# A router-and-experts stage: gathered rows that carry their weights, and a rarely taken block cut in two

## The chip, the cores and the metric

The kernel runs on one core of one Trainium2 chip. The metric is the device time of one execution in microseconds (us), taken as the median of several runs. Engine names are those of the profile: PE (matrix multiply, with PEld for its weight loads), DVE, ACT, POOL and SP; PEq, DVEq and so on are the engines' instruction sequencers.

## The reference

The program is a network over 256 tokens of width 1024: two layers of mixer and grouped mixture of experts, then two more blocks of attention, cross attention and feed-forward. The change touches the mixture of experts, which runs once in each of the first two layers:

```
def grouped_moe(h, router_w, router_b, w_gate, w_up, w_down):
    t = h.reshape(B_ * S, D)
    scores = jax.nn.sigmoid((t @ router_w).astype(jnp.float32))
    sel = scores + router_b.astype(jnp.float32)
    ...
    top_s = jnp.take_along_axis(scores, top_idx, axis=-1)
    top_w = top_s / jnp.sum(top_s, axis=-1, keepdims=True)
    combine = jnp.einsum('nk,nke->ne', top_w, jax.nn.one_hot(top_idx, N_EXPERTS, dtype=jnp.float32))
    y = jnp.zeros((t.shape[0], D), jnp.float32)
    for e in range(N_EXPERTS):
        he = jax.nn.silu(t @ w_gate[e]) * (t @ w_up[e])
        y = y + combine[:, e:e + 1] * (he @ w_down[e]).astype(jnp.float32)
```

The router picks one of four groups and two of the four experts in it. There are 16 experts with gate and up matrices of 1024 x 512 and a down matrix of 512 x 1024, all float32: 96 MB of weights in each layer.

## The kernel before

`moe(l)` (L1229) is one such stage. It normalises x into xn (two tiles of 128 tokens), splits xn into a high and a low part (xh on ACT, xl on POOL, L1274, in `parts`), computes the router's scores on PE and the choice on DVE (sel, pair, ec, gc, pick, L1291 to L1317), ranks each token within its expert (rk, L1327), and counts the tokens of each expert. The counts, as integers in the tile cnti (L1338), are read into registers, because the code branches on them. POOL also writes xn to a DRAM tile xd (L1289) from which rows are gathered later.

The experts are worked off in eight pairs p, each with room for 64 tokens of either expert. The tokens of the pairs 0 and 1 (`FIRST` is 2) are brought together by one-hot matmuls (`gather`, ph, L1374); from pair 2 on POOL gathers rows of xd by an index list (`rows`, L1419), and `columns` turns them on PE into hg. `tokens_of` (ohb, L1391) makes the one-hot masks from which `indices` computes the lists. Then `up(p)` multiplies with gate and up (pg, pu, L1474, 64 matmuls), adds the previous pair's result to x (scatter, py, L1510 and L1511), forms hd = silu(pg) * pu (L1484, L1485), transposes it, and builds the pair's placing matrix Sm and its combine weights ws in `places` (two transposes pS and four small products pw on PE, copies on ACT). `down(p)` multiplies with the down matrices (po, L1523).

A pair has twelve weight loads of 1 MB, issued by SP in program order (`fetch`, L222) into a rotation of 17 slots; each waits until its slot is free.

More than 64 tokens for an expert are handled by branches. In `more_up` and `more_down` (L1671, L1674) a pair gets a second pass for 32 further tokens of each expert; in the runs shown this happens once, in layer 0 for pair 3. Whatever still exceeds that is done by `rest` (L1609), a long block under `tc.If(left > 96)` that passes every token through every expert. It is never taken in these runs, so each engine named in it jumps over it once in each layer, in pair 5 between up and py:

```
                left = nc.values_load(cnti[0:1, 0:1], min_val=0, max_val=2 * S, engines=engines + (mybir.EngineType.SP,))
                with tc.If(left > 96):
```

PE, DVE, ACT and SP take part. Inside are both token tiles and 16 experts, 912 matmuls and transposes on PE in all, with weights fetched by SP into four slots of the rotation that are set aside for it (`self.spare`); the gate and up loads of pair 6 are issued ahead of it for that reason. What follows the block on an engine waits until the jump is over.

Of the kernel before, what the change touches and what calls it, by code (L numbers as in the profile page):

```python
# [11 lines left out]
F32 = mybir.dt.float32  # L12
# [9 lines left out]
P = 128  # L22
# [98 lines left out]
class Net:  # L121
# [99 lines left out]
    def fetch(self, raw, src, rows="(k p) n -> p k n"):  # L221
        self.nc.sync.dma_start(raw, src.rearrange(rows, p=P))  # L222
        return raw
# [1005 lines left out]
    def moe(self, l):  # L1229
# [4 lines left out]
        with self.phase(f"moe{l}", MOE_RING, True) as mp:  # L1234
# [14 lines left out]
            xh = mp.tile([P, 2, D], F32R, name="xh")  # L1249
            xl = mp.tile([P, 2, D], F32R, name="xl")  # L1250
# [28 lines left out]
            xd = self.dram.tile([S, D], F32, name="xd")  # L1279
# [9 lines left out]
            nc.gpsimd.dma_start(xd.rearrange("(t p) d -> p t d", p=P), xn)  # L1289
# [59 lines left out]
            self.split(cs, ch, cl)  # L1349
            def hot(ps, c0, n):  # L1350
# [3 lines left out]
                for t in range(2):  # L1354
                    if m == 4:
                        oh = kept[:, t, :].rearrange("p (e s) -> p e s", e=m)
                    else:
                        oh = mp.tile([P, m, n], F32R, tag=f"oh{m}{t}", name="oh")
# [5 lines left out]
            hg = []  # L1364
# [18 lines left out]
            ones_of, idx, got = [], mp.tile([P, 16], I32, name="idx"), []  # L1383
# [13 lines left out]
            def indices():  # L1397
                px = self.bank([P, 16], name="px")
                for p in range(2, 8):
                    h, q = (p - 2) // 3, (p - 2) % 3  # L1400
                    for c, n, col in ((0, 128, p), (128, 64, 8 + p)):
                        for t in range(2):
                            mm(px[0:n, col:col + 1], ones_of[2 * h + t][:, q, c:c + n], self.tok[:, t:t + 1],
                               start=t == 0, stop=t == 1)

                none = mp.tile([P, 16], F32, name="none")
                for n, c in ((P, 2), (64, 10)):
                    e = (slice(0, n), slice(c, c + 6))
                    V.tensor_scalar(none[e], px[e], 0.5, 2.0 * S, op0=ALU.is_lt, op1=ALU.mult)
                    V.scalar_tensor_tensor(idx[e], px[e], -1.0, none[e], op0=ALU.add, op1=ALU.add)  # L1410
                got.extend(mp.tile([P, 2, D], F32, tag=n, name=n) for n in ("xh", "xl"))
# [4 lines left out]
            def rows(i, p):  # L1416

                n = 64 if i else 128
                nc.gpsimd.indirect_dma_start(got[i][0:n, p % 2, :], None, xd[:, :],  # L1419
                                             bass.IndirectOffsetOnAxis(ap=idx[0:n, 8 * i + p:8 * i + p + 1], axis=0),  # L1420
                                             bounds_check=S - 1, oob_is_err=False)

            def columns(src, n, out):

                src = src.rearrange("r (b q k) -> r b k q", b=2, k=4)
                for b in range(2):
                    pt = self.bank([P, 4, n], name="hgT")
# [11 lines left out]
            def places(oh, p, r):  # L1439
# [7 lines left out]
                Sm = kept[:, 3 if r else 2, :]  # L1447
                if not r:
                    ws = mp.tile([P, 1], F32, tag="ws", name="ws", bufs=3)
                else:  # L1450
                    ws = mp.tile([P, 1], F32, tag="wsa", name="wsa")
                nc.scalar.copy(Sm, pS)  # L1452
                m = 32 if r else 64
                for i in range(P // m):
                    e = 2 * p + i % 2
                    nc.scalar.copy(ws[m * i:m * i + m, :], pw[m * i:m * i + m, e:e + 1])
                return Sm, ws

            def up(p, W, between=None):

                nonlocal oneh
                if p == 0:
                    oneh = hot((0, 1), 0, 64)
# [20 lines left out]
                nc.scalar.activation(hd, pg, AF.Silu)  # L1484
                V.tensor_tensor(hd, hd, pu, op=ALU.mult)  # L1485
# [4 lines left out]
                Sm, ws = places([oneh[t][:, q] for t in range(2)], p, 0)  # L1490
                if 1 <= p < 7:
                    columns(got[0][:, (p + 1) % 2, :], P, hg[0][:, (p + 1) % 2])
# [4 lines left out]
                if p in (1, 3, 5):  # L1497
                    oneh = hot((p + 1, p + 2), 0, 64)
                return hidT, Sm, ws

            def turn_hidden(hd, out):
                pt = self.bank([P, 4, P], name="hT")
# [47 lines left out]
            def more_up(p, W, hidT):  # L1550

                oh = hot((p,), 64, 32)
                hga = self.sp.tile([P, KD, 64], F32, tag="e1", name="hga")
                columns(got[1][0:64, p % 2, :], 64, hga)
# [6 lines left out]
                twice = self.sp.tile([P, 2, 2, 64], F32R, tag="gt", name="ohd")  # L1561
                for t in range(2):
                    V.tensor_copy(twice[:, t], oh[t].unsqueeze(1).to_broadcast([P, 2, 64]))
                Sm, ws = places([twice[:, t].rearrange("p c s -> p (c s)") for t in range(2)], p, 1)
# [32 lines left out]
            def weights(src, step, p, into=None):  # L1597
                w = I[src][l, 2 * p], I[src][l, 2 * p + 1]
                n = w[0].shape[1]
                into = [t.rearrange("p (k n) -> p k n", n=n) for t in into or [self.slot([P, 2048]) for i in range(4)]]  # L1600
# [8 lines left out]
            def rest():  # L1609


                W.extend(first_two(6))
                self.spare = [self.slot([P, 2048]) for i in range(4)]
                left = nc.values_load(cnti[0:1, 0:1], min_val=0, max_val=2 * S, engines=engines + (mybir.EngineType.SP,))
                with tc.If(left > 96):
                    n = 0
                    wv = mp.tile([P, 16], F32, name="wv")
                    ft = self.spare[0][:, 0:1024]
                    hc = self.spare[0][:, 1024:2048].rearrange("p (k n) -> p k n", n=P)
                    hid = self.spare[0][:, 0:512].rearrange("p (k n) -> p k n", n=P)  # L1620
                    for t in range(2):
                        V.tensor_scalar(wv[:, 0:2 * FIRST], rk[:, t, 0:2 * FIRST], 64.0, None, op0=ALU.is_gt)
                        V.tensor_scalar(wv[:, 2 * FIRST:], rk[:, t, 2 * FIRST:], 96.0, None, op0=ALU.is_gt)
                        V.tensor_tensor(wv, wv, cs[:, t, :], op=ALU.mult)
                        nc.sync.dma_start(ft, xd[128 * t:128 * t + 128, :])
                        columns(ft, P, hc)
                        for e in range(NE):
                            ps = []
                            for src in ("exp_w_gate", "exp_w_up"):
                                ps.append(self.bank([P, 512], name="pe"))  # L1630
                                for b in range(2):
                                    w = self.spare[1 + n % 3].rearrange("p (k n) -> p k n", n=512)
                                    n += 1
                                    self.fetch(w, I[src][l, e][512 * b:512 * b + 512, :], "(p k) n -> p k n")
                                    for k in range(4):
                                        mm(ps[-1], hc[:, 4 * b + k, :], w[:, k, :], start=b + k == 0, stop=b + k == 4)
                            hd = self.sp.tile([P, 512], F32, tag="gt", name="hde")
                            nc.scalar.activation(hd, ps[0], AF.Silu)
                            V.tensor_tensor(hd, hd, ps[1], op=ALU.mult)
                            turn_hidden(hd, hid)  # L1640
                            po = [self.bank([P, 512], name="poe") for c in range(2)]
                            for b in range(2):
                                w = self.spare[1 + n % 3].rearrange("p (k n) -> p k n", n=D)
                                n += 1
                                self.fetch(w, I["exp_w_down"][l, e][256 * b:256 * b + 256, :], "(p k) n -> p k n")
                                for k in range(2):
                                    for c in range(2):
                                        mm(po[c], hid[:, 2 * b + k, :], w[:, k, 512 * c:512 * c + 512], start=b + k == 0,
                                           stop=b + k == 2)
                            for c in range(2):  # L1650
# [815 lines left out]
```

## Time and profile before

| | |
|---|---|
| runs | 1595.86, 1598.49, 1601.05 us (median 1598.49) |
| profiled execution | 1595.95 us, span 1594.2 us |
| PE busy | 1497.0 us (94%) |
| DVE / ACT / POOL busy | 915.6 (57%) / 677.5 (42%) / 149.7 us (9%) |
| moved by DMA | 417.80 MB, mean 262 GB/s |
| expert stage of layer 0 / layer 1 | about 195 to 460 us / 600 to 850 us |

All times are us from the start of the span. In a row of the timeline, the brackets give the idle time of the engine just before, and what ended it. "PEclk" is the clock that PE was granted, as a share of full speed. A jump, a register read and a semaphore wait are no work: they show in the list of waits and under their line of the program, on the sequencers.

### The profile page before, as it was taken

The page shows a single profiled execution, that of the slowest core. Times are in us where ns is not written, and L with a number is a line of the kernel's source. Part 1 is how long each engine was busy: PE and PEld are TensorE (multiplying, and loading weights), DVE is VectorE, ACT ScalarE, POOL GpSimd, SP SyncE. Part 2 cuts the span into 40 slices and gives each one's busy share as a digit, 9 for nine tenths or more (in the row PEclk, how much of TensorE's full clock was granted, in tenths as well). Part 3 has the DMA queues.
Part 4 walks back from the last instruction along what each step waited for, and adds up shares of the span by engine and source line. Part 5 has one row for each costly group of instructions (what it writes and reads, how often), then busy time and mean ns, then how long its engine had stood idle before and what let it go on. Part 6 is the DMA issues. An engine that isn't in the chain of part 4 may idle for free.

```text
span 1594.2 us, 23071 instructions
## 1 busy us (share of the span) xinstructions
PE 1497.0 (94%) x8797; PEld 1065.8 (67%) x8797; DVE 915.6 (57%) x1773; ACT 677.5 (42%) x1417; POOL 149.7 (9%) x196
## 2 busy tenths in 40 slices
PE   6999979998989997999898999999999999999998
PEld 3666634434459974444345887788887997788886
DVE  4755533233358984223216786866667777766665
ACT  3434431111145643111115354765556666665554
POOL 0320011000000002100001100110000211110000
PEclk9999999999989998999999999999999999999999
DMA  9998989999958887999998532555644443545540
GB/s 356 349 312 297 361 334 408 420 405 385 401 185 264 292 335 296 412 419 420 416 370 270 179 108 92 171 186 172 220 163 162 160 144 95 182 162 196 200 158 27
DMA packets 171642, 417.80 MB, mean 262 GB/s; under 512 B 9588, under 2 KB 93196, under 8 KB 146928
## 3 DMA queue, kind: packets, MB, share of 16 engines
q1 hardware_dynamic: 165696, 403.46, 68.5%
q0 software_dynamic: 5536, 12.51, 2.3%
q8 instruction: 86, 1.41, 0.4%
q14 instruction: 52, 0.43, 0.1%
q10 hardware_dynamic: 272, 0.00, 0.0%
HBM read 418.79 MB, written 3.16 MB: 265 GB/s over the span
## 4 chain that ended last, share of the span: by engine, by line
PE 40%; DVE 4%; DMA 2%; ACT 2%; issue 1%; POOL 1%; DVEq 0%; POOLq 0%; SPq 0%; ACTq 0%
PE pgu L2341 9%; PE pgu L2342 5%; PE fy L383 2%; PE fy L382 2%; PE fy L381 2%; PE lin L381 2%; PE lin L382 2%; PE lin L383 2%; DMA w<-in_exp_w_up 1%; PE sc L911 1%; PE linc L381 1%; DVE hl L230 1%; PE op L383 1%; PE op L381 1%; PE linc L382 1%
## 5 line engine op out<-in xcount | busy, mean ns | idle before, releaser
L230 DVE TENSOR_TENSOR hl<-w,hl 128x1024 fp32r<-128x1024 f32 x280 | 336.1, 1233 | 51.5 <-ACT hl L229 51.3
L229 ACT CAST hl<-w 128x1024 fp32r<-128x1024 f32 x280 | 280.2, 1046 | 33.3 <-DMA w<-in_even_w_in 19.9
L2341 PE MATMUL pgu<-hT,hl 128*128 128x512 f32 x640 | 224.4, 393 | 0.0
L2342 PE MATMUL pgu<-hT,hl 128*128 128x256 f32 x640 | 178.3, 279 | 0.0
L381 PE MATMUL lin<-hl,hThi 128*128 128x256 f32 (+2 forms) x480 | 160.1, 336 | 2.4 <-ACT hl L229 1.8
L382 PE MATMUL lin<-hl,hThi 128*128 128x256 f32 (+2 forms) x480 | 154.8, 323 | 1.8 <-DVE hl L230 1.7
L383 PE MATMUL lin<-hl,hTlo 128*128 128x256 f32 (+2 forms) x480 | 153.6, 321 | 0.0
L2341 PEld LDWEIGHTS pgu<-hT,hl 128*128 128x128 f32 x640 | 120.0, 187 | 27.0
L1485 DVE TENSOR_TENSOR hd<-hd,pu 128x512 f32<-128x512 f32 x16 | 11.0, 688 | 214.2 <-PE pu L1474 214.2
L1474 PE MATMUL pg<-w,hg 128*64 128x512 f32 x512 | 117.7, 611 | 13.9 <-ACT hg L1378 10.1
L2342 PEld LDWEIGHTS pgu<-hT,hl 128*128 128x128 f32 x640 | 120.7, 189 | 2.0
L1523 PE MATMUL po<-w,hidT 128*64 128x512 f32 x512 | 116.6, 605 | 3.8 <-PEq L1674 1.8
L1474 PE MATMUL pu<-w,hg 128*64 128x512 f32 x512 | 114.3, 593 | 2.2 <-DMA w<-in_exp_w_up 2.2
L381 PEld LDWEIGHTS lin<-hl,hThi 128*128 128x128 f32 x480 | 93.4, 195 | 18.0 <-issue 7.9
L382 PEld LDWEIGHTS lin<-hl,hThi 128*128 128x128 f32 x480 | 93.6, 195 | 10.8 <-DVE hl L230 3.2
L1474 PEld LDWEIGHTS pg<-w,hg 128*64 128x64 f32 x512 | 42.4, 141 | 85.2 <-issue 58.1
L383 PEld LDWEIGHTS lin<-hl,hTlo 128*128 128x128 f32 x480 | 93.2, 194 | 7.2 <-DVE hl L230 0.8
L1474 PEld LDWEIGHTS pu<-w,hg 128*64 128x64 f32 x512 | 41.9, 137 | 71.4 <-issue 65.6
L1523 PEld LDWEIGHTS po<-w,hidT 128*64 128x64 f32 x512 | 42.9, 139 | 66.4 <-issue 61.2
L1452 ACT CAST kept<-pS 128x256 fp32r<-128x256 f32 x17 | 6.3, 373 | 170.0 <-PE pS L184 170.0
L1538 ACT CAST eo<-of 128x512 fp32r<-128x512 f32 x32 | 19.8, 617 | 115.5 <-DVE of L1535 115.2
L381 PE MATMUL linc<-hThi,hl 128*128 128x256 f32 x224 | 66.8, 298 | 0.0
(573 smaller groups left out, 2930.2 us busy)
## 6 DMA issues: line engine op xcount, KB each, us to landing
w<-in_exp_w_gate SPq DMA_DIRECT2D x64, 1024.0 KB, 15.1
w<-in_exp_w_down SPq DMA_DIRECT2D x64, 1024.0 KB, 14.5
w<-in_exp_w_up SPq DMA_DIRECT2D x64, 1024.0 KB, 15.7
w<-in_ada_w SPq DMA_DIRECT2D x48, 1024.0 KB, 7.8
w<-in_ffn_wg SPq DMA_DIRECT2D x22, 1024.0 KB, 5.5
w<-in_ffn_wu SPq DMA_DIRECT2D x22, 1024.0 KB, 7.4
w<-in_ffn_wd SPq DMA_DIRECT2D x22, 1024.0 KB, 8.7
w<-in_even_w_in SPq DMA_DIRECT2D x14, 1024.0 KB, 10.2
```

The source lines that it names most:

```text
L229: pin(self.nc.scalar.copy(w[:, 0], src))
L230: pin(self.nc.vector.tensor_tensor(w[:, 1], src, w[:, 0].bitcast(F32), op=ALU.subtract))
L381: pin(mm(out, lh, rh, start=start, stop=False))
L382: pin(mm(out, lh, rl, start=False, stop=False))
L383: pin(mm(out, ll, rh, start=False, stop=stop))
L911: pin(self.nc.tensor.matmul(p[:, os], q[:, qs], k[:, ks], start=os.start > 0, stop=False))
L1474: pin(mm(pp[64 * j:64 * j + 64, :], hg[0][:, p % 2, k, 64 * j:64 * j + 64], w[j][k // 4][:, k % 4, :], start=k == 0, stop=k == KD - 1, til ...
L1485: V.tensor_tensor(hd, hd, pu, op=ALU.mult)
L1523: pin(mm(po[c][64 * j:64 * j + 64, :], hidT[:, k, 64 * j:64 * j + 64], W[2][j][k // 2][:, k % 2, 512 * c:512 * c + 512], start=k == 0, sto ...
L1538: nc.scalar.copy(eh[c], of)
L2341: mm(pp[i], wh[:, k, :], both[:, :, k, :], start=k == 0, stop=False)
L2342: mm(pp[i][:, 0, :], wl[:, k, :], hi[:, k, :], start=False, stop=k == KD - 1)
```

## The change

1. xd is written earlier. Each token tile of xn goes to DRAM right behind its normalisation, as a DMA of its own on POOL's queue, pinned in program order, ahead of `parts`. Rows of xd have 16 further columns, into which the combine weights cs are written by a third DMA; the gathered rows bring their weights along. Gathers are 128 rows wide also for the second pass.
2. From pair 2 on `places` is replaced by `known`: Sm is one comparison on DVE of the slot numbers with the token number of each row, and ws is copied by ACT out of the gathered row. The one-hot tiles of the later pairs go.
3. `tokens_of` does three comparisons for each mask instead of two.
4. `rest` becomes two blocks, for one token tile each, in pairs 5 and 6. Their weights would be fetched by POOL into the gather tiles, so SP and the rotation have no part in them, and the loads of pair 6 are issued like all others. PE, DVE, ACT and POOL take part.
5. Silu and the product hd are pinned in program order.

```
 def fetch(self, raw, src, rows="(k p) n -> p k n", by=None):
-        self.nc.sync.dma_start(raw, src.rearrange(rows, p=P))
+        (by or self.nc.sync).dma_start(raw, src.rearrange(rows, p=P))
...
+            xd = self.dram.tile([S, D + NE], F32, name="xd")
             for t in range(2):
                 for k0 in (0, 4):
                     self.norm_cols(self.norm_turn(self.x, t, k0), hT, t, k0)
                 rs[t] = self.norm_rows(self.x, t, xn, t)
-            xd = self.dram.tile([S, D], F32, name="xd")
+                pin(nc.gpsimd.dma_start(xd[128 * t:128 * t + 128, 0:D], xn[:, t, :]))
             parts(0)
...
             parts(1)
-            nc.gpsimd.dma_start(xd.rearrange("(t p) d -> p t d", p=P), xn)
...
             self.split(cs, ch, cl)
+            nc.gpsimd.dma_start(xd[:, D:].rearrange("(t p) e -> p t e", p=P), cs)
...
-                        o = self.sp.tile([P, 3, 192], BF16, tag=("e2", "gt")[h], name="ohb")
+                        o = self.sp.tile([P, 3, 256], BF16, tag=("e2", "gt")[h], name="ohb")
...
-                        for c, n, s0 in ((0, 64, 0), (128, 32, 64)):
+                        for c, n, s0 in ((0, 64, 0), (128, 32, 64), (192, 32, 64)):
...
+            def known(p, i, Sm):
+                V.tensor_scalar(Sm, slots, number[:, 6 * i + p:6 * i + p + 1], None, op0=ALU.is_equal)
+                ws = mp.tile([P, 1], F32, tag=("ws", "wsa")[i], name="ws", bufs=(3, 1)[i])
+                m = 32 if i else 64
+                for g in range(P // m):
+                    h, e = slice(m * g, m * g + m), D + 2 * p + g % 2
+                    nc.scalar.copy(ws[h, :], got[i][h, p % 2, e:e + 1])
+                return Sm, ws
...
-                Sm, ws = places([oneh[t][:, q] for t in range(2)], p, 0)
+                Sm, ws = places([oneh[t][:, q] for t in range(2)], p) if p < FIRST else own_places.pop(0)
                 if 1 <= p < 7:
...
+                    own_places.append(known(p + 1, 0, kept[:, p % 2, :]))
...
-            def rest():
-                W.extend(first_two(6))
-                self.spare = [self.slot([P, 2048]) for i in range(4)]
-                left = nc.values_load(cnti[0:1, 0:1], min_val=0, max_val=2 * S, engines=engines + (mybir.EngineType.SP,))
+            def rest(p, t):
+                left = nc.values_load(cnti[0:1, 0:1], min_val=0, max_val=2 * S,
+                                      engines=engines + (mybir.EngineType.Pool,))
                 with tc.If(left > 96):
...
-                own = up(p, W, rest if p == 5 else None)
+                own = up(p, W, (lambda: rest(p, p - 5)) if p in (5, 6) else None)
```

The change also moves instructions on the engines, at three places.

The first is PE ahead of the gate matmuls of pair 0, where the registers are read. Each read is a TENSOR_LOAD and two ISA rows. Before there are six, then the gate matmuls; this is their end:

```order
L1669 TENSOR_LOAD cnti
L1669 ISA x2
L1669 TENSOR_LOAD cnti
L1669 ISA x2
L1474 MATMUL pg<-w,hg 64x512 x8
```

And in the changed kernel, where eight stand there, the end of them:

```order
L1612 TENSOR_LOAD cnti
L1612 ISA x2
L1665 TENSOR_LOAD cnti
L1665 ISA x2
L1612 TENSOR_LOAD cnti
L1612 ISA x2
L1665 TENSOR_LOAD cnti
L1665 ISA x2
L1479 MATMUL pg<-w,hg 64x512 x8
```

The two reads of L1612, for the two long blocks, now stand among the six of the pairs; the one read of L1614 stood before at the block itself.

The second is POOL in front of the router. Before:

```order
L496 TENSOR_TENSOR rstd<-rstd,half 128x1 x2
L1274 TENSOR_TENSOR xl<-xn,xh 128x512 x2
L1289 DMA xd<-xn 128x2x1024
L1274 TENSOR_TENSOR xl<-xn,xh 128x512 x2
L1419 DMA xh<-xd,idx 128x1024 x2
```

And in the changed kernel:

```order
L496 TENSOR_TENSOR rstd<-rstd,half 128x1
L1280 DMA xd<-xn 128x1024
L496 TENSOR_TENSOR rstd<-rstd,half 128x1
L1280 DMA xd<-xn 128x1024
L1273 TENSOR_TENSOR xl<-xn,xh 128x512 x4
L1350 DMA xd<-cs 128x2x16
L1419 DMA xh<-xd,idx 128x1040 x2
```

All four xl subtractions now stand behind both writes of xd, and the second write needs the second tile of xn.

The third is DVE at the long block of pair 5. Before:

```order
L1671 UNCONDITIONAL_BRANCH x2
L1485 TENSOR_TENSOR hd<-hd,pu 128x512
L1614 TENSOR_LOAD cnti
L1615 COMPARE_AND_BRANCH
L1622 TENSOR_SCALAR wv<-rk 128x4
```

And in the changed kernel:

```order
L1667 UNCONDITIONAL_BRANCH x2
L1612 TENSOR_LOAD cnti
L1614 COMPARE_AND_BRANCH
L1620 TENSOR_SCALAR wv<-rk 128x4
L1621 TENSOR_SCALAR wv<-rk 128x12
```

The jump no longer stands behind hd, which needs pu; hd comes behind the block.

## Rows read from the trace of the kernel before

**Rows 1.** The windows: us; busy us (x instructions) of PE, PEld, DVE, ACT, POOL; PEclk, DMA share, GB/s
```profile
220.00:230.00 10.00, 9.21 (x42) 4.19 (x44) 0.00 (x0) 3.60 (x7) 0.00 (x0) 0.81 0.34 119
390.00:400.00 10.00, 7.00 (x28) 5.66 (x30) 4.79 (x8) 1.74 (x7) 0.00 (x0) 0.66 0.58 225
790.00:800.00 10.00, 9.70 (x48) 3.72 (x46) 2.80 (x4) 1.24 (x2) 0.00 (x0) 1.00 0.85 350
800.00:810.00 10.00, 10.00 (x53) 5.12 (x50) 2.91 (x5) 0.60 (x1) 0.00 (x0) 1.00 0.71 274
830.00:840.00 10.00, 8.59 (x42) 4.00 (x38) 2.74 (x5) 0.00 (x0) 0.00 (x0) 1.00 1.01 422
```

**Rows 2.** The timeline of PE: start, length, engine, line, operation, tiles, [idle before]
```profile
220.79 1.97 PE L1474 MATMUL pg<-w,hg 128*64 128x512 f32 x4 [5.82 <-ACT hg L1378]
```

**Rows 3.** The timeline of ACT in the same stretch
```profile
218.82 1.93 ACT L1378 ACTIVATE hg<-ph,ab 128x256 f32<-128x256 f32 x4 [2.39 <-DMA xd<-xn]
```

**Rows 4.** Line 1669, 212 to 224: ns min/median/max, first and last start us
```profile
L1669 PEldq SEQ_ASSERT  x6: 18/18/28, 217.1 to 220.7; - x6
```

**Rows 5.** The timeline of DVE, the router's chain of layer 0
```profile
206.78 0.28 DVE L1298 TENSOR_TENSOR ec<-sel 128x128 f32<-128x128 f32 x1
...
207.64 1.51 DVE L1298 TENSOR_TENSOR gc<-gs 128x32 f32<-128x32 f32 x1
209.08 1.55 DVE L1299 TENSOR_TENSOR gc<-gs 128x32 f32<-128x32 f32 x1
...
216.11 0.16 DVE L1338 CAST cnti<-cnt 1x8 int32<-1x8 f32 x1
```

**Rows 6.** The timeline of PE, pairs 4 to 6 of layer 0
```profile
346.69 2.80 PE L1474 MATMUL pg<-w,hg 128*64 128x512 f32 x12 [0.34 <-PEq L1671]
...
372.49 4.08 PE L1474 MATMUL pg<-w,hg 128*64 128x512 f32 x18 [0.31 <-PEq L1671]
...
383.67 2.77 PE L1474 MATMUL pu<-w,hg 128*64 128x512 f32 x12
392.71 0.76 PE L1510 MATMUL py<-eo,kept 128*128 128x512 f32 x1 [6.26 <-DVEq L1615]
...
406.97 2.37 PE L1474 MATMUL pg<-w,hg 128*64 128x512 f32 x10 [0.30 <-PEq L1671]
```

**Rows 7.** Line 1615, 375 to 400: columns as in rows 4
```profile
L1615 PEldq COMPARE_BRANCH  x1: 6013/6013/6013, 382.4 to 382.4; - x1
...
L1615 DVEq COMPARE_BRANCH  x1: 56/56/56, 387.0 to 387.0; - x1
...
L1615 DVEq EVENT_SEMAPHORE  x1: 21/21/21, 392.5 to 392.5; - x1
```

**Rows 8.** The waits of PE in 595 to 865 (layer 1): us, times, longest
```profile
PE py L1510 <- DVEq L1615: 6.3, 1, 6.3
...
PE pu L1474 <- DMA w<-in_exp_w_up: 2.2, 2, 1.4
```

**Rows 9.** The timeline of SP's queue, layer 1
```profile
781.96 0.33 SPq L222 DMA_DIRECT2D w<-in_exp_w_gate  x1
801.92 2.03 SPq L222 DMA_DIRECT2D w<-in_exp_w_down  x4
```

**Rows 10.** The waits of PE in 190 to 470 (layer 0): us, times, longest
```profile
PE pg L1474 <- PEq L1671: 1.2, 4, 0.3
...
PE po L1523 <- DMA w<-in_exp_w_up: 0.6, 2, 0.3
```

**Rows 11.** The timeline of POOL, layer 0
```profile
207.35 3.22 POOL L1274 TENSOR_TENSOR xl<-xn,xh 128x512 fp32r<-128x512 f32 x2 [0.57 <-ACT xh L1273]
```

**Rows 12.** Groups by shape of DVE, 212 to 217: busy us, mean ns
```profile
L1391 DVE TENSOR_TENSOR ohb<-rk,kt 128x192 bf16<-128x192 f32 x4 | 1.4, 339 | 0.0
```

**Rows 13.** The timeline of PE, pair 4 of layer 0
```profile
363.02 0.27 PE L184 MATMUL pS<-kt,kept 128*128 128x128 f32 x1
...
363.58 1.23 PE L184 MATMUL hgT<-kt,xh 128*128 128x128 f32 x8
```

More of the change, by code (lines that the diff above doesn't have):

```diff
@@ L1247, in moe @@
             sc = mp.tile([P, 2, 16], F32, name="sc")
-            xh = mp.tile([P, 2, D], F32R, name="xh")
-            xl = mp.tile([P, 2, D], F32R, name="xl")
+            xh, xl = (mp.tile([P, 2, D + NE], F32R, tag=n, name=n)[:, :, 0:D] for n in ("xh", "xl"))
             lg, rs = {}, {}
@@ L1362, in hot @@
                 return ohs
-            hg = []
+            hg, own_places = [], []
             def gather(k0, k1):
@@ L1397, in indices @@
             def indices():
-                px = self.bank([P, 16], name="px")
+                px = self.bank([P, 14], name="px")
                 for p in range(2, 8):
                     h, q = (p - 2) // 3, (p - 2) % 3
-                    for c, n, col in ((0, 128, p), (128, 64, 8 + p)):
+                    for c, col in ((0, p), (128, 6 + p)):
                         for t in range(2):
-                            mm(px[0:n, col:col + 1], ones_of[2 * h + t][:, q, c:c + n], self.tok[:, t:t + 1],
+                            mm(px[:, col:col + 1], ones_of[2 * h + t][:, q, c:c + 128], self.tok[:, t:t + 1],
                                start=t == 0, stop=t == 1)
[L1406 to L1411, printed above, removed]
+                none = mp.tile([P, 14], F32, name="none")
+                V.tensor_copy(number[:, 2:], px[:, 2:])
+                V.tensor_scalar(none[:, 2:], number[:, 2:], 0.5, 2.0 * S, op0=ALU.is_lt, op1=ALU.mult)
+                V.scalar_tensor_tensor(idx[:, 2:], number[:, 2:], -1.0, none[:, 2:], op0=ALU.add, op1=ALU.add)
+                for n in ("xh", "xl"):
+                    got.append(mp.tile([P, 2, D + NE], F32, tag=n, name=n))
+                    V.memset(got[-1][:, :, D:], 0.0)
                 rows(0, 2)
@@ L1437, in columns, with places @@
                                              bias=self.ab[:, 1, b, k:k + 1])
-            def places(oh, p, r):
+            def places(oh, p):
                 pS = self.bank([P, 256], name="pS")
@@ L1446, in places @@
                     mm(pw, oh[t], cl[:, t, :], start=False, stop=t == 1)
[L1447 to L1451, printed above, removed]
-                nc.scalar.copy(Sm, pS)
[L1453 to L1456, printed above, removed]
+                Sm = kept[:, 2, :]
+                ws = mp.tile([P, 1], F32, tag="ws", name="ws", bufs=3)
+                nc.scalar.copy(Sm, pS)
+                for j in range(2):
+                    h = slice(64 * j, 64 * j + 64)
+                    nc.scalar.copy(ws[h, :], pw[h, 2 * p + j:2 * p + j + 1])
+                return Sm, ws
[6 more added lines that the diff above has]
+                    nc.scalar.copy(ws[h, :], got[i][h, p % 2, e:e + 1])
                 return Sm, ws
             def up(p, W, between=None):
-                nonlocal oneh
                 if p == 0:
-                    oneh = hot((0, 1), 0, 64)
+                    oneh.extend(hot((0, 1), 0, 64))
                     gather(0, 4)
@@ L1496, in up, with turn_hidden @@
                         rows(0, p + 3)
-                if p in (1, 3, 5):
-                    oneh = hot((p + 1, p + 2), 0, 64)
                 return hidT, Sm, ws
-            def turn_hidden(hd, out):
-                pt = self.bank([P, 4, P], name="hT")
+            def turn_hidden(hd, out, bank=None):
+                pt = bank.rearrange("p (k n) -> p k n", k=4) if bank is not None else self.bank([P, 4, P], name="hT")
                 src = hd.rearrange("p (b q k) -> p b k q", b=2, k=2)
@@ L1550, in more_up @@
             def more_up(p, W, hidT):
-                oh = hot((p,), 64, 32)
                 hga = self.sp.tile([P, KD, 64], F32, tag="e1", name="hga")
-                columns(got[1][0:64, p % 2, :], 64, hga)
+                columns(got[1][0:64, p % 2, 0:D], 64, hga)
                 pp = self.bank([P, 512], name="pgu")
@@ L1560, in more_up @@
                            start=k == 0, stop=k == KD - 1, tile_position=(0, 32 * i))
[L1561 to L1564, printed above, removed]
+                Sm, ws = known(p, 1, kept[:, 3, :])
                 hd = self.sp.tile([P, 512], F32, tag="gt", name="hda")
@@ L1595, in moe, with weights @@
             engines = (mybir.EngineType.PE, mybir.EngineType.DVE, mybir.EngineType.Activation)
-            def weights(src, step, p, into=None):
+            def weights(src, step, p):
                 w = I[src][l, 2 * p], I[src][l, 2 * p + 1]
                 n = w[0].shape[1]
-                into = [t.rearrange("p (k n) -> p k n", n=n) for t in into or [self.slot([P, 2048]) for i in range(4)]]
+                into = [self.slot([P, 2048]).rearrange("p (k n) -> p k n", n=n) for i in range(4)]
                 cut = [(j, k0) for k0 in range(0, w[0].shape[0], step) for j in range(2)]
@@ L1615, in rest @@
                 with tc.If(left > 96):
-                    n = 0
[L1617 to L1641, printed above, removed]
-                            for b in range(2):
[L1643 to L1650, printed above, removed]
-                                sl = slice(512 * c, 512 * c + 512)
-                                of = self.sp.tile([P, 512], F32, tag="gt", name="ofe")
-                                V.scalar_tensor_tensor(of, po[c], wv[:, e:e + 1], gate[:, sl], op0=ALU.mult, op1=ALU.mult)
-                                V.tensor_tensor(self.x[:, t, sl], self.x[:, t, sl], of, op=ALU.add)
@@ L1656, in moe @@
-            oneh, W = None, []
+                    wv = mp.tile([P, 16], F32, tag="wv", name="wv")
+                    space = [e.rearrange("p a d -> p (a d)")[:, 0:2048] for e in got]
+                    hc = hg[0][:, (p + 1) % 2]
+                    hid = self.sp.tile([P, 4, P], F32, tag="e1", name="hide")
+                    banks = [self.bank([P, 512], name="be") for i in range(6)]
+                    V.tensor_scalar(wv[:, 0:2 * FIRST], rk[:, t, 0:2 * FIRST], 64.0, None, op0=ALU.is_gt)
@@ new lines, in rest, with fetched @@
+                    V.tensor_scalar(wv[:, 2 * FIRST:], rk[:, t, 2 * FIRST:], 96.0, None, op0=ALU.is_gt)
+                    V.tensor_tensor(wv, wv, cs[:, t, :], op=ALU.mult)
+                    nc.gpsimd.dma_start(space[0][:, 0:D], xd[128 * t:128 * t + 128, 0:D])
+                    columns(space[0][:, 0:D], P, hc, banks[0:2])
+                    n = 0
+                    def fetched(src, nd):
+                        nonlocal n
+                        n += 1
+                        return self.fetch(space[n % 2].rearrange("p (k n) -> p k n", n=nd), src, "(p k) n -> p k n", nc.gpsimd)
@@ new lines, in rest @@
+                    for e in range(NE):
+                        for i, src in enumerate(("exp_w_gate", "exp_w_up")):
+                            for b in range(2):
+                                w = fetched(I[src][l, e][512 * b:512 * b + 512, :], 512)
+                                for k in range(4):
+                                    mm(banks[2 + i], hc[:, 4 * b + k, :], w[:, k, :], start=b + k == 0, stop=b + k == 4)
+                        hd = self.sp.tile([P, 512], F32, tag="gt", name="hde")
+                        nc.scalar.activation(hd, banks[2], AF.Silu)
+                        V.tensor_tensor(hd, hd, banks[3], op=ALU.mult)
+                        turn_hidden(hd, hid, banks[0])
+                        for b in range(2):
+                            w = fetched(I["exp_w_down"][l, e][256 * b:256 * b + 256, :], D)
+                            for k in range(2):
+                                for c in range(2):
+                                    mm(banks[4 + c], hid[:, 2 * b + k, :], w[:, k, 512 * c:512 * c + 512], start=b + k == 0,
+                                       stop=b + k == 2)
+                        for c in range(2):
+                            sl = slice(512 * c, 512 * c + 512)
+                            of = self.sp.tile([P, 512], F32, tag="gt", name="ofe")
+                            V.scalar_tensor_tensor(of, banks[4 + c], wv[:, e:e + 1], gate[:, sl], op0=ALU.mult, op1=ALU.mult)
+                            V.tensor_tensor(self.x[:, t, sl], self.x[:, t, sl], of, op=ALU.add)
@@ L1657, in moe @@
+                    for i, q in ((0, p + 1), (1, p + 1), (0, p + 2)):
+                        if q < 8:
+                            rows(i, q)
             for p in range(8):
-                if p != 6:
-                    W = first_two(p)
-                    self.spare = None
-                W = W[-2:] + [weights("exp_w_down", 256, p, self.spare)]
+                W = first_two(p) + [weights("exp_w_down", 256, p)]
                 if p == 7:
```

25 lines of the change are left out of this document (11 added, 14 removed).

## The prediction

> **What bounds the kernel now.** I read the windows first, to see which engine each stretch of the two expert stages leaves idle, then what PE waited for there, then the instructions around each wait. PE has 94% of the span, so time can only come out of PE's own work or out of the places where PE stands. In the expert stages there are three.
>
> The first is the start. In 220 to 230 PE is busy 9.2 of 10 us at a granted clock of 0.81, and the DMA share is only 0.34 [rows 1]. PE's last gather matmul is followed by 5.82 us of nothing before the gate matmuls begin at 220.79 [rows 2]. The row blames ACT's hg, which itself waited 2.39 us for the xd write that still reads xn [rows 3]. But PE's sequencer is reading registers in just that time: six reads of cnti, their last parts from 217.1 to 220.7, 0.72 us apart [rows 4]. So two things end together at 220.7, and removing one of them leaves the other. The reads start when DVE has written cnti at 216.27 [rows 5].
>
> The second is the jump over the long block. PE's up matmuls of pair 5 end at 386.44 and the next matmul is at 392.71, 6.26 us later, "<-DVEq L1615" [rows 6]. What takes long is the jump itself: COMPARE_BRANCH on PE lasts 6.01 us, and DVE's, at 387.0, is only left at 392.5 [rows 7]. PE's sequencer runs ahead of the array (its branch begins at 382.4, 4.0 us before the array runs dry), so its own jump ends at 388.4 and costs 2.0; DVE's jump, begun behind hd's product, costs the other 4.2. Pair 4's gate matmuls start at 346.69, pair 5's at 372.49, pair 6's at 406.97 [rows 6]: an ordinary pair takes 25.80 us, the one with the jump 34.48. The jump is worth 8.7 us: 6.3 of standing and 2.4 of half clock behind it (granted clock 0.66 in 390 to 400 [rows 1]).
>
> The third is the weights in layer 1. Loads of 1024 KB at 422 GB/s [rows 1] take 2.5 us each, so the twelve of a pair take 30 us, and PE works them off in 25.8. Seventeen slots cover this for some pairs; in the end PE waits 2.2 us for up weights [rows 8]. SP stands at the block until its last load has landed: no load is issued between 781.96 and 801.92 [rows 9], and the queue runs dry (274 GB/s in 800 to 810 [rows 1]). Layer 0 is different: there PE's longest wait for a weight is 0.3 us [rows 10]. **Layer 0 is bound by PE, layer 1 ends bound by its loads.**
>
> **The parts of the change, for one execution.**
>
> Rows written early. The two half writes of xd go out before the xl subtractions, so hg no longer waits for them. On their own they earn nothing: the register reads end at the same moment. They move work, though. POOL's queue now holds both writes ahead of all four xl, and the second write waits for the second half of xn. Today two xl run before the router's chain on DVE and two (3.22 us, 1.6 each) beside it [rows 11], and there two tiny operations, gc, take 1.51 and 1.55 us where ec, four times as large, takes 0.28 [rows 5]. That is 2.7 us lost to two xl. With all four beside the chain, from about 205.2 to 211.6, DVE gets one operation through per xl (sel and the three pair); what is left, from ec at 206.78 to cnti at 216.27, is 9.5 us today less those 2.7. So cnti is written near 218.4: +2.1, between 0 (the chain begins behind the xl) and +2.8 (a second loss as large as today's).
>
> Four more small ohb operations stand ahead of cnti on DVE: 4 x 0.34 [rows 12] = +1.4. Two more register reads stand on PE ahead of the gate matmuls: 2 x 0.72 = +1.4. The longer idle time lets more of the gate matmuls run at half clock: today some 3.8 of 10 us in 220 to 230 (a mean of 0.81 between 0.5 and 1), so +0.5, between 0 and 1.7. **The start costs +5.4 in each layer** (2.8 to 7.3). The first slot comes free with the gate matmuls, so the loads start later by the same amount.
>
> The combine weights in the rows. A write of 16 KB and wider, 128-row gathers ride on POOL's queue, and the rows are used a pair later. I take 0: that pair's 25.8 us is the cover.
>
> Places by comparison. From pair 2 on PE no longer does the two transposes and four small products: 363.02 to 363.58, 0.56 us a pair [rows 13], six pairs, -3.4. In the one extra block that runs (layer 0, pair 3) another such set goes, and ACT's copies of weights that take its place stand ahead of its next operand; I take -0.6, one set. The comparison is DVE work of 256 columns, like the one-hot operations it replaces, a pair ahead of its use: 0.
>
> The long block in two parts. In DVE's program its jump now stands before hd's product, directly behind the previous branch, so it runs while PE still does gate and up. SP no longer takes part; POOL does, with its gathers for the next two pairs already issued. What is left is PE's own jump, twice. The register read ahead of it is gone (0.4). How long a jump over half the block takes, no row tells. Over the whole block, 912 matmuls, it takes 6.01 [rows 7]; at the short branches PE stands 0.3 [rows 10]. Read as a price by distance, half the block is 3.0 us, which lies wholly inside the sequencer's lead of 4.0, and both jumps would be free: 0 instead of 8.7. Read as a price for leaving what is at hand, it is 6.0 again, twice, of which 2.0 - 0.4, and 0.2 for the join, 1.8 in all, stands in the open. I take the second, because the 6.0 on PE and the 5.5 on DVE are nearly the same though DVE's block has far fewer instructions. [...] Clock: behind layer 1's wait of 1.4 for weights [rows 8] it stays at 1.00 [rows 1], behind the 6.3 it fell. For 1.8, near the lower of these, I add 0.9 each, between 0 and 2.4. Two jumps cost 5.4 in place of 8.7: **-3.3 in layer 0** (from -8.7, both free, to +8.7, each as dear as today's one).
>
> In layer 1 PE's gains sit ahead of loads that end later, so only the loads count. SP's drain is gone: 350 and 274 GB/s instead of 422 in 790 to 810 [rows 1] are 2.2 MB, **-5.2**. One set of places, that of pair 7, lies behind the last wait: -0.6.
>
> **Sum.** Layer 0: 5.4 - 3.4 - 0.6 - 3.3 = -1.9. Layer 1: 5.4 - 5.2 - 0.6 = -0.4. Together -2.3 on the profiled execution's 1595.95, that is 1593.7. The median of the three runs shown, 1598.49, is 2.5 above that execution; carried to it, the forecast is **1596.2**.
>
> **Rivals.** All times are carried to the median.
>
> *The jumps are free.* If half the block is near enough, or PE's sequencer leads by more than today, layer 0 keeps all of 8.7: -2.3 - 5.4 = -7.7, 1590.8. For it: the lead of 4.0 covers any jump up to 4 us. Against it: DVE's and PE's jumps cost alike over blocks of different length. With the start at its lower bound too, 2.6 less in each layer, it is -12.9, 1585.6.
>
> *Each jump costs what the one costs now (slower).* The place is the first py behind each block. If PE's sequencer gets to the branch with little left in the array, because the last up weights have only just landed, or if another engine that py depends on comes late out of its jump, each block costs 8.7 instead of 2.7, in layer 0 alone: -2.3 + 12.0 = +9.7, 1608.2. It decides where the lead falls towards 0. For it: today most of the wait was for another engine's jump, and POOL is new at the block. Against it: DVE is past its jump early, and layer 0 hardly waits for loads.
>
> *The queue was not held.* If SP would have stood for slots in 782 to 802 anyway, taking the block off it earns nothing, and layer 1 keeps its later start: -2.3 + 5.2 = +2.9, 1601.4. Against it: four loads go out in 2.03 us as soon as SP is let go [rows 9], so slots were free.
>
> **How the numbers follow.** The forecast has 0.35, free jumps 0.33, dear jumps 0.20, no gain from the queue 0.12. A measurement of this kernel can tell 0.3%, 4.8 us, from no change. The forecast's own range, by the bounds of start and clock, is 1591 to 1601; it is faster by more than 0.3% 1 time in 4 and slower 1 in 20. Free jumps are faster by more 17 times in 20, dear jumps slower 9 in 10, the last 1 in 6. That makes faster 0.37, slower 0.22, same 0.41. The range reaches from free jumps with a cheap start to dear jumps: 1586 to 1608.
>
> **What would show it.** Right: gate matmuls that begin some 5 us later after the start of each expert stage, behind eight register reads and no wait for xd; small operations of the router chain stretched to 1.5 us four times; two gaps on PE of about 2 us before py or up at pairs 5 and 6, named after PE's own sequencer and not after DVE; loads in layer 1 without the pause from 782 to 802; no pS from pair 2. Wrong: gaps of 0.3 (free), gaps of 6 (dear), or gate matmuls that begin no later than today.

## The result and the profile after

The changed kernel takes 1614.22 us (median of four runs, 1612.2 to 1617.59), the kernel before 1598.72 in the same comparison: a ratio of 1.010, 95% interval 1.0073 to 1.0127. The forecast was 1596.2 in a range of 1586 to 1608. It was wrong, in sign too: 15.5 us slower where 2.3 less was forecast.

Three landmarks show where the time went: in each expert stage the first rstd on DVE (of the normalisation that opens the stage), the first gate matmul of pair 0, and the end of pair 7's down matmuls (the last row's start and length added). All are rows of the timelines; the sums are mine.

| stretch, us | before | after | change | forecast |
|---|---|---|---|---|
| layer 0, first rstd to first gate matmul | 24.13 | 28.61 | +4.5 | +5.4 |
| layer 0, first gate matmul to last down matmul | 236.54 | 243.10 | +6.6 | -7.3 |
| layer 1, first rstd to first gate matmul | 23.84 | 28.48 | +4.6 | +5.4 |
| layer 1, first gate matmul to last down matmul | 222.22 | 224.62 | +2.4 | -5.8 |

That is +18.1 in the two stages. The spans of the two profiled executions differ by 21.6; the other 3.5 lie outside the stages, and the profiled execution of the changed kernel is the slowest of its four runs.

What PE waits for in layer 0 of the changed kernel (us, times, longest):

```profile
PE hT L184 <- DVE hd L1490: 11.2, 8, 1.6
PE pg L1479 <- issue: 6.0, 1, 6.0
PE pr L1323 <- DVE pick L1317: 5.5, 1, 5.5
...
PE py L1514 <- PEq L1614: 1.8, 1, 1.8
...
PE pu L1479 <- PEq L1614: 1.0, 1, 1.0
```

The first line is new. The wait of 6.3 for DVE's jump [rows 6] is gone; PE's own two jumps, 1.8 and 1.0, stand in its place. In layer 1 the same line for hd reads 11.2, 8 again, the jumps cost 2.5 and 1.7, and the wait for up weights [rows 8] is gone.

DVE's timeline in pair 4 of the changed kernel shows where hd stands:

```profile
371.40 1.28 DVE L1517 TENSOR_TENSOR x<-x,py 128x512 f32<-128x512 f32 x2 [12.43 <-PE py L1515]
372.60 0.68 DVE L1490 TENSOR_TENSOR hd<-hd,pu 128x512 f32<-128x512 f32 x1
374.19 0.69 DVE L1510 COPY hidT<-hT 128x512 f32<-128x512 f32 x1 [0.91 <-PE hT L184]
```

And PE's, in the same pair:

```profile
370.64 0.50 PE L1514 MATMUL py<-eo,kept 128*128 128x512 f32 x1
370.98 0.39 PE L1515 MATMUL py<-eo,kept 128*128 128x512 f32 x1
371.20 0.40 PE L1514 MATMUL py<-eo,kept 128*128 128x512 f32 x1
371.44 0.40 PE L1515 MATMUL py<-eo,kept 128*128 128x512 f32 x1
373.43 0.72 PE L184 MATMUL hT<-kt,hd 128*128 128x128 f32 x4 [1.59 <-DVE hd L1490]
```

DVE has been idle for 12.43 us when the first py arrives. hd's product needs only the Silu, which ACT ends 6 us before, and pu, which is done when the first py starts at 370.64, but it stands behind two additions that need the four py. They run at 371.40, hd at 372.60, and PE, which has worked off its four py, waits 1.59 us for it before hT. This repeats in pairs 1 to 7 of both layers; the eighth wait, in pair 0, is 0.2. Behind some of these waits the granted clock falls as well: it is 0.83 in 850 to 860 (0.50 in 856 to 859, behind a wait of 1.60), in pair 7 of layer 1, which has no long block, where the kernel before has 1.00 in its pair 7 [rows 1]; in pair 4, in 370 to 380, it stays at 1.00.

The windows of the changed kernel that answer to [rows 1]:

```profile
220.00:230.00 10.00, 4.03 (x12) 1.38 (x12) 0.89 (x7) 2.08 (x5) 0.75 (x1) 0.67 0.17 67
...
790.00:800.00 10.00, 6.46 (x34) 3.87 (x32) 5.04 (x9) 1.50 (x4) 0.98 (x1) 1.00 1.02 415
800.00:810.00 10.00, 9.69 (x46) 3.67 (x44) 3.08 (x5) 1.61 (x4) 0.00 (x0) 1.00 1.01 419
```

The start is later (4.0 us of PE work in 220 to 230 instead of 9.2), and the loads of layer 1 run without a pause: 415 and 419 GB/s in 790 to 810, where they had fallen to 350 and 274. The stage starts 15.5 us later in this execution, so these windows hold other work; but from 770 to 850 no window of 10 us is below 413 GB/s.

### The profile page after: what moved, and what is told of

Its sections match the earlier page's. It is cut to its first block, busy times and chain, and to the rows that moved or that the text cites. A ratio compares the mean times of both kernels' runs of the same rounds, so it can differ in the third digit from the quotient of the medians.

```text
span 1615.8 us, 22948 instructions
## 1 busy us (share of the span) xinstructions
PE 1494.5 (92%) x8719; PEld 1055.0 (65%) x8719; DVE 920.7 (57%) x1780; ACT 673.9 (42%) x1404; POOL 152.6 (9%) x200
## 5 line engine op out<-in xcount | busy, mean ns | idle before, releaser
L1517 DVE TENSOR_TENSOR x<-x,py 128x512 f32<-128x512 f32 x68 | 44.0, 683 | 188.2 <-PE py L1515 188.2
L1479 PE MATMUL pg<-w,hg 128*64 128x512 f32 x512 | 117.4, 610 | 15.8 <-issue 12.3
L1436 ACT ACTIVATE hg<-hgT,ab 128x128 f32<-128x128 f32 x48 | 18.0, 456 | 122.5 <-PE hgT L184 122.4
```

The costliest lines, as they stand in the source:

```text
L1436: nc.scalar.activation(out[:, k, :], pt[:, k, :], AF.Identity, scale=self.ab[:, 0, b, k:k + 1], bias=self.ab[:, 1, b, k:k + 1])
L1479: pin(mm(pp[64 * j:64 * j + 64, :], hg[0][:, p % 2, k, 64 * j:64 * j + 64], w[j][k // 4][:, k % 4, :], start=k == 0, stop=k == KD - 1, til ...
L1517: V.tensor_tensor(xs, xs, py, op=ALU.add)
```

## The experiments

The theory is that two pins (a pin holds an instruction behind everything that the program writes before it on its engine), which stand last in the list of the change and do not show what they move, cost 11 us of waiting in each layer, and that the rest of the change is worth about what was forecast. The rival is that the later start and the two jumps are dearer than forecast, and that the waits for hd only stand in for others.

**Only the pins taken away (e9_no_pins).**

```
-                pin(nc.scalar.activation(hd, pg, AF.Silu))
-                pin(V.tensor_tensor(hd, hd, pu, op=ALU.mult))
+                nc.scalar.activation(hd, pg, AF.Silu)
+                V.tensor_tensor(hd, hd, pu, op=ALU.mult)
```

> The changed kernel with nothing undone but the two pins: Silu and hd's product stand where the change wrote them, and the scheduler is free to place them. It puts hd's product ahead of the two scatter additions in every pair, and in pairs 5 and 6 behind the long block. Theory A (the pins, and nothing else of the change, cost the 11 us in each layer): no wait of hT for hd, and the time of e1_hd_first within 0.2%, 1592 to 1599. Rival B (the pins were needed to get DVE's jump off the path): waits of 6.3 us for DVEq at pairs 5 and 6, 1603 or more.

Measured: 1595.67 us, ratio to the kernel before 0.999 (0.9977 to 1.0002). Of the waits for hd only the 0.2 of pair 0 is left in each layer, and DVE's timeline in pair 4 has the product first again:

```profile
364.73 0.69 DVE L1490 TENSOR_TENSOR hd<-hd,pu 128x512 f32<-128x512 f32 x1 [11.85 <-PE pu L1479]
365.34 1.28 DVE L1517 TENSOR_TENSOR x<-x,py 128x512 f32<-128x512 f32 x2
```

The waits at the blocks stay PE's own (2.0 at one of them in layer 0), so the pins were not needed to get DVE's jump out of the way. The two lines are the whole loss: 1614.22 to 1595.67, 18.6 us.

**The pins kept, the product written first (e1_hd_first).**

```
-                if self.pending:
-                    self.pending(2)
                 hd = self.sp.tile([P, 512], F32, tag="e1", name="hd")
                 pin(nc.scalar.activation(hd, pg, AF.Silu))
                 pin(V.tensor_tensor(hd, hd, pu, op=ALU.mult))
+                if self.pending:
+                    self.pending(2)
```

> The changed kernel with Silu and hd's product written ahead of the two scatter additions of the previous pair, and still pinned; nothing else moves. Theory A (the product pinned behind the two additions keeps PE waiting 1.5 to 1.6 us before every hT of pairs 1 to 7, 11.2 us in each layer): the fourteen waits of hT for hd go, and the time falls by 15 to 22 us, to 1593 to 1599. In layer 1 not all of it need come back, since the loads end close behind. Rival B (the added time is the later start and the two jumps, and the waits for hd only stand in for other waits): it falls by 5 us at most, to 1609 or more, and other waits take the place of those for hd.

Measured: 1595.4 us, ratio 0.9984 (0.9972 to 0.9996). So it is the place of the product and not the pin as such. Of 22 us of waits some 19 come back: from the first gate to the last down matmul layer 0 falls by 12.3 us, layer 1 by 5.5 only, since there PE now waits for up weights again (3.5 us in three waits). With hd's waits in place, PE had been slow enough for the loads.

**The other way round: the kernel before with the product late (e2_before_hd_late).** In pair 5 it keeps its place.

```
-                nc.scalar.activation(hd, pg, AF.Silu)
-                V.tensor_tensor(hd, hd, pu, op=ALU.mult)
+                late = pin if p != 5 else (lambda i: i)
+                late(nc.scalar.activation(hd, pg, AF.Silu))
+                late(V.tensor_tensor(hd, hd, pu, op=ALU.mult))
```

> The kernel before with Silu and hd's product pinned behind the scatter additions, in all pairs but 5 (there the order stays). Theory A: six waits of hT for hd of 1.6 us in each layer (pairs 1 to 4, 6 and 7), 9.6 us and a few us of half clock behind them in layer 0; in layer 1 they sit ahead of loads that end late anyway, so that 1.6 to 9.6 us show. Together 1598 + 12 to 20, 1610 to 1618. Rival B: under 5 us, below 1603, since DVE's additions would only move from behind the product to ahead of it.

Measured: 1621.1 us, ratio 1.0145 (1.0127 to 1.0164), 22.8 above its own 1598.31. The line of waits, for layer 0:

```profile
PE hT L184 <- DVE hd L1486: 10.5, 7, 1.6
```

The sign is the theory's, the size above its upper end: pair 0 waits too (1.4 in each layer), which I had not counted. From the first gate to the last down matmul layer 0 grows by 13.1 us and layer 1 by 6.9, so a third of layer 1's 10.5 does not show; PE's 2.2 us of waits for up weights [rows 8] are gone there.

**No long block (e3_no_block), and shorter ones (e4_short_blocks).** Both start from e1_hd_first; in the first `rest` returns behind its register read, in the second its loop runs over fewer experts:

```
-                    for e in range(NE):
+                    for e in range(((8, 4), (3, 2))[l][t]):
```

> As e1_hd_first, without the two long blocks (the count is still read); it leaves out what tokens past the second pass would get, which no token needs here. Theory A (a jump costs 6 us on PE's sequencer whatever its distance, of which 1 to 2.5 us stand in the open, with some half clock): 3 to 6 us less than e1_hd_first, all of it in layer 0 if layer 1 is bound by its loads; pairs 5 and 6 of layer 0 take about 25.3 us each. Rival B (the jumps over half a block are nearly free): within 1 us of e1_hd_first.

> As e1_hd_first, with fewer experts in the long blocks, that no execution here enters: 8 and 4 in layer 0 (232 and 120 matmuls and transposes), 3 and 2 in layer 1 (92 and 64); it leaves out the other experts there. Theory A (the jump's price is that of leaving what is at hand): COMPARE_BRANCH on PE lasts about 6 us at 232 and at 120, and falls to 0.3 only at a size near that of the second pass's block (44). Rival B (a price by distance, 6.0 us at 456): about 3.1, 1.6, 1.2 and 0.8 us.

Measured without the blocks: 1587.98 us, 7.4 less than e1_hd_first, a little above the upper end of what was expected, and not all of it in layer 0: by the landmarks 6.8 there and 1.9 in layer 1. Pair 5 of layer 0 takes 25.23 us, gate to gate, against 30.86 in the profile of e1_hd_first (29.26 in e9_no_pins). Over an ordinary pair, pairs 5 and 6 take 6.1 (e9_no_pins) to 8.0 us (e1_hd_first) more, so the two jumps cost 6 to 8 us together: not much less than the one that they replace, 8.7.

The shorter blocks took 1593.22 us (a single run). PE's COMPARE_BRANCH lasts there, in order of time at 232, 120, 92 and 64 matmuls (ns min/median/max, first and last start us, one answer for each stretch):

```profile
L1614 PEldq COMPARE_BRANCH  x1: 6025/6025/6025, 383.5 to 383.5; - x1
...
L1614 PEldq COMPARE_BRANCH  x1: 5997/5997/5997, 410.4 to 410.4; - x1
...
L1614 PEldq COMPARE_BRANCH  x1: 320/320/320, 768.1 to 768.1; - x1
...
L1614 PEldq COMPARE_BRANCH  x1: 333/333/333, 797.9 to 797.9; - x1
```

It is a step, not a slope: 6.0 us at 120 matmuls as at 456 (5.88 to 6.13 in the changed kernel) and at 912 [rows 7], 0.3 at 92. That the two small blocks stand in layer 1 is not the reason, since the jumps over 456 take 5.88 and 6.05 there in the changed kernel. Between 92 and 120 nothing was measured, and no run shows what makes the step.

The size of the block is not all, though. The next branch on PE behind the first long jump of layer 0 is the short one of the second pass, L1670, and in e1_hd_first it takes nearly as long as the long one:

```profile
L1670 PEldq COMPARE_BRANCH  x1: 5074/5074/5074, 391.6 to 391.6; - x1
```

PE stands 2.5 us at it; this is part of the 8.0. Behind the second jump of layer 1 PE stands another 1.8 us in e1_hd_first and 2.8 in e9_no_pins, for which the trace names no cause ("issue"). In the changed kernel the short branch takes 2.50 us and PE's longest wait for it is 0.3; in the kernel before it takes 0.45, with the short blocks 0.25. No run here shows what makes it dear.

**The start, in four steps.** The kernel before took 1597.73 us beside these four and 1598.31 beside e1_hd_first, so 0.6 us of each difference from e1_hd_first is not the edit's. e5_late_rows, from e1_hd_first, writes xd where the kernel before does:

```
-                pin(nc.gpsimd.dma_start(xd[128 * t:128 * t + 128, 0:D], xn[:, t, :]))
...
             parts(1)
+            nc.gpsimd.dma_start(xd[:, 0:D].rearrange("(t p) d -> p t d", p=P), xn)
```

> As e1_hd_first, with xd written where the kernel before writes it, in one DMA behind the first two xl subtractions; the weights' columns stay as changed. Theory A (the early writes push all four xl beside the router's first operations, and sel waits 5.1 us for them): sel takes 0.2 us again, two gc take 1.5 each as before, cnti comes about 2 us earlier and so do the gate matmuls, in both layers: 3 to 4.5 us less than e1_hd_first, 1591 to 1592.5. Rival B (the rows written early are what the start needs, hg now waits for the late write): no gain, or 2 to 4 us more.

Measured: 1592.47 us, ratio 0.9966 (0.9952 to 0.9981), 2.9 less than e1_hd_first, just short of the 3 to 4.5 expected; the intervals of the two overlap, so it is the landmarks that show the gain. The first gate matmul comes 26.59 and 26.27 us after the first rstd, where it was 28.65 and 28.53. Writing the rows early costs 2 us in each layer and gains nothing. The cause, in the changed kernel on POOL and on DVE:

```profile
206.62 5.96 POOL L1273 TENSOR_TENSOR xl<-xn,xh 128x512 fp32r<-128x512 f32 x4
```

```profile
207.50 5.13 DVE L1291 TENSOR_TENSOR sel<-sc,rbias 128x32 f32<-128x32 f32 x1 [0.30 <-ACT sc L1288]
```

sel, 32 elements a partition, takes 5.13 us: it ends at 212.63, when the last of the four xl is through (212.58). In e5_late_rows it takes 0.19.

e6_counts_first, from e1_hd_first, holds ohb behind cnti on DVE (`one` is the comparison, `counted` the copy into cnti):

```
+                            tc.add_manual_dep(one.ins, counted.ins.name,
+                                              mybir.DependencyInfo(mybir.DependencyClass.NoSync, mybir.DependencyReason.DATA),
+                                              reason="counts first")
```

> As e1_hd_first, with the twelve ohb comparisons held behind cnti on DVE. Theory A (the eight register reads behind cnti hold the gate matmuls): cnti comes some 4 us earlier, the reads run while the array still does the gather, the gate matmuls then wait for hg alone and start 3.5 to 4 us earlier after the stage's first rstd (28.6 us in the changed kernel, 24 to 25.2 here): 6 to 8 us less than e1_hd_first over both layers, 1587.5 to 1589.5. Rival B (hg or the clock holds them, not the reads): under 2 us.

Measured: 1587.17 us, ratio 0.9926 (0.9905 to 0.9947), 8.2 less than e1_hd_first; gate matmuls at 24.71 and 24.67 us. So the register reads behind cnti held them, and still do. This is the end of the reads in layer 0, columns as in [rows 4]; the gate matmuls start at 221.96:

```profile
L1668 PEldq SEQ_ASSERT  x6: 18/18/32, 216.9 to 221.9; - x6
```

The kernel before has the same order, with eight comparisons ahead of cnti.

e7_counts_late_rows does both.

> Both: counts first, and xd written where the kernel before writes it. Theory A: the reads end about 22.5 us after the first rstd, and hg, which again waits for the late write of xd, ends at about 24.1 as in the kernel before, so the gate matmuls start there: within 1 us of e6_counts_first in each layer, not the sum of the two gains. Rival B (the gains add): 10 to 12 us less than e1_hd_first, 1584 to 1585.

Measured: 1584.93 us, ratio 0.9913 (0.9896 to 0.993); gate matmuls at 22.72 and 22.08 us, "<-ACT hg". That is 2.0 and 2.6 earlier than in e6_counts_first, where I had expected no more than 1; by the landmarks the gains add. (The run times of the two overlap.) What I had wrong shows on ACT and PE in layer 0:

```profile
219.46 1.93 ACT L1377 ACTIVATE hg<-ph,ab 128x256 f32<-128x256 f32 x4 [4.86 <-DMA xd<-xn]
```

```profile
220.41 5.35 PE L1482 MATMUL pg<-w,hg 128*64 128x512 f32 x16 [3.00 <-ACT hg L1377]
```

The gate matmuls do not wait for the last of the four hg, which ends at 221.39, but start 0.95 us after the first begins. The last register read ends at 220.3 and holds them even here. In the kernel before, then, hg [rows 3] would have let them go at least 1 us before 220.79 [rows 2], and the reads alone [rows 4] held them: the prediction's reading, that the two end together, was wrong.

e8_all reads the block's count once for both blocks.

> As e7_counts_late_rows, with the count for the long blocks read once for both, seven reads on PE in place of eight. Theory A (hg ends last at the start): the gate matmuls start where they do there, within 0.5 us in each layer, no difference that can be measured. Rival B (the reads still end last): 0.7 us earlier in each layer, 1.4 less.

Measured: 1581.67 us, ratio 0.9896 (0.9877 to 0.9915), the fastest here: 1% below the kernel before, 2% below the changed one. The reads now end at 218.4, and the gate matmuls, behind hg alone, start 0.2 us earlier than in e7_counts_late_rows (22.50 and 21.93 us after the first rstd), in layer 0 0.6 us behind the start of the first hg at 218.66:

```profile
219.27 3.68 PE L1482 MATMUL pg<-w,hg 128*64 128x512 f32 x8 [3.41 <-ACT hg L1377]
```

So the 3.3 us to e7_counts_late_rows are not explained by the start; its five runs and the six of this kernel overlap (1581.72 to 1585.04 and 1578.05 to 1585.75), and I do not count them as a gain of that read.

## Why the prediction was wrong

The step that failed is in the part on the long block: "In DVE's program its jump now stands before hd's product, directly behind the previous branch, so it runs while PE still does gate and up." That is right, but the program says two things about the place of the product, and I read only one. It stands behind the block, and it also stands behind the two additions of py. I costed the move of the product at nothing and named no cover for it, in all sixteen pairs, not only at the blocks. It costs 1.5 to 1.6 us in each of fourteen pairs, some 19 us in all by e1_hd_first and e9_no_pins. The pins stood in the list of the change, and no term of the sum was theirs.

The rest, by the terms of the sum, in the changed kernel:

- *The start, +5.4 a layer*: +4.5 and +4.6. The chain up to pick lost 2.1 as said (pick starts 16.81 us after the first rstd, before 14.72), though by one operation that waits for all four xl (sel, 5.13 us) and not by four that wait for one each. From pick to cnti +1.1, where 1.4 was taken. The two register reads +1.4. The 0.5 of half clock for the longer idle time did not show: the first 16 gate matmuls take 5.77 us behind 5.97 of idle time in layer 0, before 5.15 behind 5.82, but 5.17 behind 6.34 in layer 1, before 5.94 behind 4.30, and pair 0 takes 27.65 us from its first gate matmul in layer 0, before 27.81 (27.04 and 30.30 in layer 1).
- *Places, 0.56 a pair*: an ordinary pair in e9_no_pins takes 25.22 us, before 25.80. Right. The further -0.6 for the extra block is not settled: pairs 2 and 3 of layer 0 take 72.65 us together before, 72.01 in e9_no_pins and 70.15 in e1_hd_first, where their own two sets are worth 1.1; PE's wait for hga in that block grows from 1.1 to 1.9 in all of the changed kernels.
- *The jumps, -3.3 in layer 0*: the price of 6.0 each, the same over 456 matmuls (5.88 to 6.13) as over 912 (6.01), is right, as is the sequencer's lead that hides most of it (4.5 us in pair 5: the branch starts at 393.2, the array runs dry at 397.67). In the changed kernel pairs 5 and 6 are 3.0 and 2.0 us above its ordinary pair (26.96), 5.0 where 5.4 was taken. Without hd's waits they cost more, 6 to 8; the short branch that became dear behind the first of them (5.07 us in e1_hd_first) is a cost that no term had.
- *The drain, -5.2 in layer 1*: the queue no longer pauses, and its rate is the one forecast. In the changed kernel the gain is lost, because PE, held by hd, no longer needs it. In e1_hd_first 3.1 us of the stretch are gained and in e9_no_pins 0.9, of 5.8 forecast: in e1_hd_first PE stands 2.8 us at each jump and waits 3.5 for weights, in e9_no_pins 2.9, 2.7 and 4.7.

So none of the three rivals came true. Jumps were not free, nor as dear as the old one, and the queue had been held. The forecast, 1596.2, is what the kernels with the product ahead measure (e9_no_pins 1595.67, e1_hd_first 1595.4). That is in part luck: the start was taken too dear, and the jumps and the drain too well, and by the landmarks the two stages together take 2.0 us more in e9_no_pins and 0.4 more in e1_hd_first than before, where 2.3 less was forecast.

## What to carry to other kernels

A pin fixes an instruction behind everything written before it on its engine: read what that is, in every repetition, and price the wait of whoever needs the result. DVE's 12.43 us of idle time in pair 4 were no cover for hd's product: what stood ahead of it waited for py, which came after pu. And the jump over a long block that is never entered lasts as long on PE over 120 matmuls (6.00 us) as over 912 (6.01) here, so cutting the block in two bought that price twice; what paid is that DVE's jump left PE's way: the wait of 6.3 us for it is gone.

## What the runs showed of the hardware

sel on DVE waited for four POOL operations here and not only for the one that ran. Against four xl back to back, in the changed kernel, it takes 5.13 us and ends when the last is through (212.63 and 212.58). Against two back to back, in the kernel before and in e5_late_rows, two gc take 1.51 and 1.54 or 1.55 in layer 0, one xl each (3.22 and 3.23 for two); sel, ahead of them, takes 0.19. Why one operation gets through between two xl and the other does not, no run shows, nor what holds either of them.

PE's jump takes 5.9 to 6.5 us over 120, 232, 456 and 912 matmuls and 0.3 over 92 and 64. The short branch L1670 right behind such a jump took 5.07 us in e1_hd_first and 2.50 in the changed kernel, against 0.45 in the kernel before.
